# Strassen's scheme for the input projections of the feed-forward stage: seven products of quarters in place of eight

## The chip, the cores and the metric

The kernel runs on one core of a Trainium2 chip. The metric is the time of one execution on the device, in microseconds (us); lower is better. The five engines are named as the profile names them: PE (TensorE, matrix products; PEld is its loading of weights), DVE (VectorE), ACT (ScalarE), POOL (GpSimd) and SP (SyncE, which here only issues transfers). Every engine works through its own list of instructions in order and waits on semaphores for the others.

## What is computed

The reference is one block of a hybrid model on 512 tokens of 1024 features, in float32. Three mixers (a gated linear recurrence, an RWKV-7 layer and a latent attention) are merged, and a gated feed-forward stage follows. Only that last stage is touched:

```python
h = rms_norm(x, ffn_pre_g[l])
gate, up = jnp.split(h @ w_ffn_in[l], 2, axis=-1)
x = x + rms_norm((jax.nn.silu(gate) * up) @ w_ffn_out[l], ffn_post_g[l])
```

Here `h` is 512 x 1024, `w_ffn_in` is 1024 x 5632 (2816 columns of gate, then 2816 of up), and `w_ffn_out` is 2816 x 1024.

## The kernel before

**Three products for one.** Each float32 operand is split into a high part, rounded to the format `float32r` in which PE takes it, and a low part, the rest. `mm3` (L134 to L139) then issues three matmuls for one: high by high (L137), high by low (L138), low by high (L139). The tokens' operand `h` is split once and stays on the chip (`self.h`: eight tiles `xH` and eight `xL`, each 128 features x 512 tokens). The weights are split as they come: `slab` (L196) loads 256 KB into a staging tile `wsD`, ACT casts it to the high tile `whD` (L205), and DVE subtracts for the low tile `wlD` (`split_low`, L132). `wsD`, `whD` and `wlD` have three buffers each, so at most three slabs of weights are ready or in use.

**The streaming loop.** `stream` (L210) takes 256 columns of weights, that is two feature tiles of 128, against all 1024 features of the input: four slabs, and for each of them two columns x two feature rows x three matmuls of 512 tokens, 12 matmuls in all. The results gather in two tiles `mmD` of the accumulation memory (PSUM), of which the pool `pD` has four. A helper, `lane`, gives instructions a priority class; the order on each engine is then made when the program is built, by a list scheduler that simulates the engines. Lane 0 is the most urgent.

**The stage in question** is `ffn` (L1240). It has eleven pairs of feature tiles (22 tiles of 128 make 2816). For each pair a stream of gate columns and one of up columns are run, 96 matmuls of 512 tokens. Then comes the gating: ACT takes a tanh of the gate (L1256), DVE forms (1 + tanh) x gate (L1257) and the product with up (L1261), ACT writes the high part `fH` (L1262) and DVE the low part `fL` (L1263). The first pair is different: its four streams take half of the tokens each (256), so that it can start while `h` for the other half is still being made by the stage ahead (`to_fm`: transposes on PE at L357, `xH` on ACT at L360, `xL` on DVE at L361).

**What follows** is `project` (L1205) with `w_ffn_out`: slabs of 128 rows x 512 columns through the same `slab` (staging tiles `wsD` again), accumulated in four tiles `po`. Beside it the residual `x1` is loaded from memory (L1281) into tiles called `xH0` to `xH7` in the pool `hp`, which are the buffers of the high tiles of `h`, so those loads wait until the last matmul that reads `h` is done. The gain `gp` is loaded at the start of `ffn` (L1246 and L1247).

Outside this stage POOL does small work: a token (L149) per group of matmuls, which paces the streams of the earlier stages and is off in `ffn`, powers for the norms (L279), and a few elementwise operations in the mixers (L594, L717).

## Time and profile before

| | |
|---|---|
| median of 3 runs | 1403.33 us (1401.97 to 1404.83) |
| the profiled execution, whole | 1408.42 us |
| its span, first to last instruction | 1406.6 us |
| granted clock of PE over the span | 0.996 |
| PE busy | 1354.8 us (96%) |
| DVE busy | 848.3 us (60%) |
| ACT busy | 638.6 us (45%) |
| POOL busy | 190.8 us (14%) |

A busy time is the time in which at least one instruction of the engine runs. PE's matmuls overlap: each is shown with its own length, and the next one starts well before it ends, so what a matmul costs is read from the distance of starts, not from its length. In the rows of groups, `out<-in` names the tiles without their buffer numbers, then the shapes, the count, the busy time and the mean length in ns, and at the end the idle time of the engine ahead of these instructions with what ended it. A timeline row has the start in us, the length in us, the engine, the line, the operation and, as xN, how many instructions were merged into the row.

### The profile page before, as it was taken

Reading aid. Unit: us, or ns where it says so; the run is one execution under the profiler, and the core shown is the slowest. Engines: PE = TensorE matmul, PEld = TensorE weight load, DVE = VectorE, ACT = ScalarE, POOL = GpSimd, SP = SyncE. Lnnn points to the kernel's source line nnn. Section 1 sums busy time; section 2 is a strip of 40 time slices with the busy share of each in tenths; the row PEclk is TensorE's granted clock in tenths of the full one; section 3 lists DMA queues with packets and bytes.
Section 4 is the critical chain, followed back from the end, with each engine's and each line's share of the span. In section 5 each row is a group of like instructions: output and inputs, shape, how many; then the busy total and the mean of one; then the engine's idle time right before and its main releaser. Section 6 shows DMA issues by size and latency. Waiting matters only on the chain.

```text
span 1406.6 us, 27356 instructions
## 1 busy us (share of the span) xinstructions
PE 1354.8 (96%) x9664; PEld 1103.2 (78%) x9664; DVE 848.3 (60%) x1756; ACT 638.6 (45%) x1259; POOL 190.8 (14%) x1042
## 2 busy tenths in 40 slices
PE   6999999999999999999999999999999999999998
PEld 5777777777777777888788888877888888888886
DVE  5567797797787784575665576655575344343234
ACT  5554546556556453433665354443354333332222
POOL 2122132131222311242210000001010000000000
PEclk9999999999999999999999999999999999999999
DMA  5565467557755777986464555415544333334233
GB/s 180 149 193 144 129 183 227 178 153 218 213 157 155 242 237 227 356 277 208 137 204 147 157 178 168 130 53 173 198 139 135 98 97 92 102 95 156 97 98 105
DMA packets 196025, 231.62 MB, mean 165 GB/s; under 512 B 42672, under 2 KB 137392, under 8 KB 195888
## 3 DMA queue, kind: packets, MB, share of 16 engines
q1 hardware_dynamic: 194496, 226.72, 52.1%
q10 hardware_dynamic: 1392, 3.15, 0.7%
q8 instruction: 76, 1.25, 0.4%
q14 instruction: 61, 0.50, 0.1%
HBM read 169.65 MB, written 60.16 MB: 163 GB/s over the span
## 4 chain that ended last, share of the span: by engine, by line
PE 82%; DMA 6%; DVE 4%; issue 4%; ACT 3%; POOL 1%; SPq 1%; POOLq 0%; DVEq 0%; ACTq 0%
PE mmD L137 18%; PE mmD L138 17%; PE mmD L139 17%; PE po L137 4%; PE po L139 4%; PE po L138 4%; PE pr L194 1%; DMA wsD<-in_w_in_dram 1%; DMA z<-zst 1%; DMA zr<-z 1%; PE pmo L1138 1%; PE pm L137 1%; PE pm L139 1%; PE pm L138 1%; PE ph L843 1%
## 5 line engine op out<-in xcount | busy, mean ns | idle before, releaser
L137 PE MATMUL mmD<-xH,whD 128*128 128x512 f32 (+1 forms) x1232 | 486.2, 397 | 11.9 <-POOL token L149 5.6
L138 PE MATMUL mmD<-xL,whD 128*128 128x512 f32 (+1 forms) x1232 | 474.2, 386 | 0.0
L139 PE MATMUL mmD<-xH,wlD 128*128 128x512 f32 (+1 forms) x1232 | 469.6, 385 | 0.9 <-DVE wlD L132 0.9
L132 DVE TENSOR_TENSOR wlD<-wsD,whD 128x512 fp32r<-128x512 f32 x384 | 263.2, 687 | 292.0 <-ACT whD L205 276.0
L205 ACT CAST whD<-wsD 128x512 fp32r<-128x512 f32 x384 | 236.7, 618 | 375.8 <-PE mmD L138 244.1
L137 PEld LDWEIGHTS mmD<-xH,whD 128*128 128x128 f32 x1232 | 232.0, 189 | 65.2 <-POOL token L149 8.9
L139 PEld LDWEIGHTS mmD<-xH,wlD 128*128 128x128 f32 x1232 | 232.2, 189 | 48.6 <-DVE wlD L132 2.0
L138 PEld LDWEIGHTS mmD<-xL,whD 128*128 128x128 f32 x1232 | 233.5, 190 | 40.1
L149 POOL MEMSET token<- 1x1 f32 x912 | 82.2, 90 | 675.4 <-PE mmD L139 660.1
L139 PE MATMUL po<-whD,fL 128*128 128x512 f32 x176 | 68.6, 390 | 0.0
L138 PE MATMUL po<-wlD,fH 128*128 128x512 f32 x176 | 68.6, 390 | 0.0
L137 PE MATMUL po<-whD,fH 128*128 128x512 f32 x176 | 61.9, 390 | 0.0
L279 POOL TENSOR_TENSOR rrs<-rtm,mhalf 128x1 f32<-128x1 f32 x8 | 4.4, 551 | 402.3 <-DVE rtm L274 368.7
L646 DVE TENSOR_TENSOR invtmp<-inv 64x30 f32<-64x30 f32 (+14 forms) x120 | 38.7, 322 | 17.7 <-DMA inv<-Ld 16.0
L594 POOL TENSOR_SCALAR BK<-BK,gC 128x128 f32<-128x128 f32 x56 | 47.0, 854 | 11.8 <-PE pr L194 11.8
L237 ACT COPY zst<-mmD 128x512 f32<-128x512 f32 x64 | 37.3, 583 | 14.6 <-PE mmD L139 14.4
L647 DVE TENSOR_TENSOR inv<-inv,invtmp 64x30 f32<-64x30 f32 (+14 forms) x120 | 38.4, 320 | 2.2
L139 PEld LDWEIGHTS po<-whD,fL 128*128 128x128 f32 x176 | 33.0, 188 | 7.0
L138 PEld LDWEIGHTS po<-wlD,fH 128*128 128x128 f32 x176 | 33.0, 188 | 7.0
L137 PEld LDWEIGHTS po<-whD,fH 128*128 128x128 f32 x176 | 33.0, 188 | 7.0
L843 PEld LDWEIGHTS ph<-hq,hk 128*32 128x32 f32 x1536 | 17.6, 111 | 18.0 <-issue 9.6
L1136 ACT COPY mpT<-pmt 128x128 f32<-128x128 f32 (+3 forms) x32 | 13.6, 425 | 38.0 <-PE pmt L1134 37.9
(349 smaller groups left out, 1960.1 us busy)
## 6 DMA issues: line engine op xcount, KB each, us to landing
wsD<-in_w_in_dram SPq DMA_DIRECT2D x176, 256.0 KB, 3.4
wsD<-in_w_ffn_in_dram SPq DMA_DIRECT2D x96, 256.0 KB, 2.8
z<-zst SPq DMA_DIRECT2D x63, 256.0 KB, 3.3
rwd<-G SPq DMA_DIRECT2D x28, 512.0 KB, 5.5
G<-rwd SPq DMA_DIRECT2D x28, 512.0 KB, 6.7
wsD<-in_w_branch_dram SPq DMA_DIRECT2D x48, 256.0 KB, 2.9
wsD<-in_w_ffn_out_dram SPq DMA_DIRECT2D x44, 256.0 KB, 2.6
zr<-z SPq DMA_DIRECT2D x26, 256.0 KB, 3.3
```

Of the source, the lines that this page charges most:

```text
L132: (eng or self.nc.vector).tensor_tensor(dst, src, high.bitcast(F32), op=ALU.subtract)
L137: first = mm(ps, lhsT=lh, rhs=rh, start=start, stop=False)
L138: mm(ps, lhsT=lh, rhs=rl, start=False, stop=False)
L139: return first, mm(ps, lhsT=ll, rhs=rh, start=False, stop=stop)
L149: token = self.nc.gpsimd.memset(self.token, 0.0).ins
L194: last = c()
L205: nc.scalar.copy(h, st)
L237: self.nc.scalar.copy(st[:m], ps)
L594: Pl.tensor_scalar(BK[:, c], BK[:, c], gC[:, c + 1:c + 2], None, op0=ALU.mult)
L646: V.tensor_tensor(tv, cv, rv, op=ALU.mult)
L647: V.tensor_tensor(U[:, :j, j + 1:], U[:, :j, j + 1:], tv, op=ALU.add)
L843: mm(g[b:b + HB, o // P, :], lhsT=k[:, t], rhs=q[:, t], start=True, stop=True)
```

## The change

The first pair stays as it was (moved to `ffn_first`, with other scratch tiles). The other ten pairs are each computed as one 2 x 2 block product: the rows of the block are gate and up (256 columns of weights each), the inner index is the lower and upper half of the 1024 features, and the columns are the two halves of the tokens. Winograd's form of Strassen's scheme takes seven products of quarters where the plain form has eight, with sums of weights (s1 to s4), sums of tokens' operands (T1 to T4) and sums of the results. Each product is 512 features x 256 columns by 256 tokens: two slabs, each with 12 matmuls of 256 tokens.

- `ffn_sides` forms T1 to T4 once: POOL adds high and low parts back (16 operations of 128x256), DVE subtracts four times (128x1024), and the results are split again by ACT and DVE. T4 is written over the right halves of the first four `h` tiles. Its scratch tiles are the buffers into which the weights of the first Strassen pair are then loaded (tags `wg0`, `wg1`, `wu0`, `wu1`).
- `ffn_seven` runs once per pair. It loads the four quarters of the weights, 512 KB each, into four tiles of which only `wu0` has two buffers. POOL forms s1 to s4 (four operations of 128x1024). Then come seven products, each with ACT's cast and DVE's split of two slabs, seven sums of results on DVE with one operand in PSUM, a copy on ACT, and the gating in two halves of the tokens, whose product with up is now on POOL.
- The results' sums lie in the staging tiles `wsD`. The gain `gp` and what `project` needs now come from a pool `fo`, opened when the tiles of the Strassen pairs are closed.

```diff
-        for f in range(0, KF, 2):
-            ts_ = [self.t(fp, [P, S], f"ft{j}", bufs=2) for j in range(2)]
...
-            if f:
-                self.stream(wg, self.h, gate)
-                self.stream(wu, self.h, up)
...
+            self.ffn_first(fH, fL, win)
+            T = self.ffn_sides(fin)
+            for f in range(2, KF, 2):
+                self.ffn_seven(fin, fH, fL, win, T, f)
+        fo = es.enter_context(tc.tile_pool(name="fo", bufs=1))
+        gp = self.t(fo, [P, D], "gp")
...
+    def ffn_sides(self, fin):
...
+                    Pl.tensor_tensor(q[:, j], self.h[0][4 * k + j][:, c].bitcast(F32),
+                                     self.h[1][4 * k + j][:, c].bitcast(F32), op=ALU.add)
...
+        def side(n, dst, a, b):
+            V.tensor_tensor(dst, a, b, op=ALU.subtract)
...
+            A.copy(h, dst)
+            self.split_low(l, dst, h)
...
+        side(1, B[0, 0], B[0, 1], B[0, 0])
+        side(3, B[0, 1], B[1, 1], B[0, 1])
+        side(2, B[1, 1], B[1, 1], B[0, 0])
+        side(4, B[1, 0], B[1, 1], B[1, 0])
...
+    def ffn_seven(self, fin, fH, fL, win, T, f):
...
+        a11, a21, a22, a12 = load("wg0", 0, 0), load("wu0", 1, 0, 2), load("wu1", 1, 1), load("wg1", 0, 1)
+        s1, s2, s4 = (self.t(fin, [P, 4, 2 * P], n) for n in ("ws1", "ws2", "ws4"))
+        Pl.tensor_tensor(s1, a21, a22, op=ALU.add)
+        Pl.tensor_tensor(s2, s1, a11, op=ALU.subtract)
+        s3 = a21
+        Pl.tensor_tensor(s3, a11, a21, op=ALU.subtract)
+        Pl.tensor_tensor(s4, a12, s2, op=ALU.subtract)
...
+        def product(w, x):
+            ps = self.t(self.pD, [P, 2, N], "mmD")
+            for k0 in range(0, 4, 2):
+                h, l = (self.t(self.wd, [P, 2, 2 * P], t, F32R, 3) for t in ("whD", "wlD"))
...
+                A.copy(h, w[:, k0:k0 + 2])
+                self.split_low(l, w[:, k0:k0 + 2], h)
...
+            A.activation(t, gate, AF.Tanh, scale=0.5)
+            V.scalar_tensor_tensor(t, t, 1.0, gate, op0=ALU.add, op1=ALU.mult)
+            Pl.tensor_tensor(t, t, up, op=ALU.mult)
+            A.activation(fH[:, f:f + 2, tok], t, AF.Copy, scale=0.5)
+            V.scalar_tensor_tensor(fL[:, f:f + 2, tok], t, 0.5, fH[:, f:f + 2, tok].bitcast(F32),
+                                   op0=ALU.mult, op1=ALU.subtract)
...
+        soon(A.copy, m1, product(a11, b11))
+        add(u2, m1, product(s2, t2))
+        m4 = product(a22, t4)
+        m5 = product(s1, t1)
+        add(u3, u2, product(s3, t3))
+        add(c22, u3, m5)
+        soon(V.tensor_tensor, u3, u3, m4, op=ALU.subtract)
+        add(u2, u2, m5)
+        add(m1, m1, product(a12, b21))
+        gated(0, m1, u3)
+        add(u2, u2, product(s4, b22))
+        gated(1, u2, c22)
```

Called in this order, the seven products are named P1 (a11), P2 (s2), P3 (a22), P4 (s1), P5 (s3), P6 (a12) and P7 (s4) below.

**Where the order moves.** Line numbers of rows of the changed kernel are its own: L1366 and L132 are the cast and the split of a Strassen slab, L1351 to L1355 the four sums of weights, L1384 the sums of results, L1392 to L1395 the gating, L1346 the loads of weights, L1263 the loads of `x1`.

DVE, in the middle of the stage, before: the row of splits, with the gating of one pair among them (`ft` is the gating's scratch, `mmD` the tile in PSUM).

```order
L132 TENSOR_TENSOR wlD_14015<-wsD_14012,whD_14014 128x512
L1263 SCALAR_TENSOR_TENSOR fL_12699<-ft_2490_13813,fH_12698 128x512
L132 TENSOR_TENSOR wlD_14033<-wsD_14030,whD_14032 128x512
L132 TENSOR_TENSOR wlD_14057<-wsD_14054,whD_14056 128x512
L132 TENSOR_TENSOR wlD_14075<-wsD_14072,whD_14074 128x512
L1257 SCALAR_TENSOR_TENSOR ft_2519_13972<-ft_2519_13972,mmD_13974 128x512
L132 TENSOR_TENSOR wlD_14093<-wsD_14090,whD_14092 128x512
L1257 SCALAR_TENSOR_TENSOR ft_2520_13973<-ft_2520_13973,mmD_13975 128x512
```

DVE at the same place in the changed kernel, from the first split of one pair (P1, of `wg_2540`) to the sum with its P2; `ws_2545` is s2, `wu_2542` is a22, `zst` is the gating's scratch of the pair before it, `c` and `wsD` hold sums of results.

```order
L132 TENSOR_TENSOR wlD_14158<-wg_2540_14137,whD_14157 128x512
L132 TENSOR_TENSOR wlD_14174<-wg_2540_14137,whD_14173 128x512
L1392 SCALAR_TENSOR_TENSOR zst_14091<-zst_14091,wsD_13882 128x512
L1384 TENSOR_TENSOR wsD_13883<-wsD_13883,mmD_14097 128x512
L132 TENSOR_TENSOR wlD_14192<-ws_2545_14146,whD_14191 128x512
L132 TENSOR_TENSOR wlD_14208<-ws_2545_14146,whD_14207 128x512
L1392 SCALAR_TENSOR_TENSOR zst_14131<-zst_14131,wsD_13883 128x512
L1395 SCALAR_TENSOR_TENSOR fL_12699<-zst_14091,fH_12698 128x2x256
L132 TENSOR_TENSOR wlD_14226<-wu_2542_14141,whD_14225 128x512
L132 TENSOR_TENSOR wlD_14242<-wu_2542_14141,whD_14241 128x512
L1384 TENSOR_TENSOR wsD_14153<-wsD_14152,mmD_14190 128x512
L1395 SCALAR_TENSOR_TENSOR fL_12699<-zst_14131,fH_12698 128x2x256
```

A pair has 25 DVE operations now where it had 14, and the last gating steps of one pair stand among the splits of the next: the split for P3 comes behind `fL` of the pair before.

POOL, the last four rows of the stage ahead and the first of the final norm, before: nothing lies between them.

```order
L279 TENSOR_TENSOR nrs_12523<-ntm_12522,mhalf 128x1
L279 TENSOR_TENSOR nrs_12636<-ntm_12635,mhalf 128x1
L279 TENSOR_TENSOR rrs_12628<-rtm_12627,mhalf 128x1
L279 TENSOR_TENSOR nrs_12636<-ntm_12635,mhalf 128x1
L279 TENSOR_TENSOR rrs_15396<-rtm_15395,mhalf 128x1
```

POOL between these places in the changed kernel, for one pair in the middle of the stage: the sums s1 to s4 of a pair (`ws_2592`, `ws_2593`, `wu_2589`, `ws_2594`), and the gating products (`zst`) around them.

```order
L1393 TENSOR_TENSOR zst_14091<-zst_14091,wsD_13884 128x512
L1393 TENSOR_TENSOR zst_14131<-zst_14131,c_2502_13885 128x512
L1351 TENSOR_TENSOR ws_2592_14415<-wu_2589_14409,wu_2590_14411 128x1024
L1352 TENSOR_TENSOR ws_2593_14416<-ws_2592_14415,wg_2588_14407 128x1024
L1354 TENSOR_TENSOR wu_2589_14409<-wg_2588_14407,wu_2589_14409 128x1024
L1355 TENSOR_TENSOR ws_2594_14417<-wg_2591_14413,ws_2593_14416 128x1024
L1393 TENSOR_TENSOR zst_14361<-zst_14361,wsD_14154 128x512
L1393 TENSOR_TENSOR zst_14401<-zst_14401,c_2550_14155 128x512
```

All four sums of the next pair stand ahead of the two gating products of the current one (`zst_14361` belongs to the pair whose splits are shown above).

SP, from the end of the stage on, before: the loads of `w_ffn_out` and of `x1` alternate.

```order
L201 DMA wsD_14637<-in_w_ffn_out_dram 128x512
L201 DMA wsD_14655<-in_w_ffn_out_dram 128x512
L1281 DMA xH_2639_14612<-x1d 128x512
L1281 DMA xH_2640_14613<-x1d 128x512
L201 DMA wsD_14673<-in_w_ffn_out_dram 128x512
L1281 DMA xH_2641_14614<-x1d 128x512
L1281 DMA xH_2642_14615<-x1d 128x512
```

SP at the same place in the changed kernel, from the last load of a quarter of `w_ffn_in` on.

```order
L1346 DMA wg_2783_15493<-in_w_ffn_in_dram 128x4x256
L1263 DMA xH_2829_15763<-x1d 128x512
L1263 DMA xH_2830_15764<-x1d 128x512
L1263 DMA xH_2831_15765<-x1d 128x512
L1263 DMA xH_2832_15766<-x1d 128x512
L1263 DMA xH_2833_15767<-x1d 128x512
L1263 DMA xH_2834_15768<-x1d 128x512
L1263 DMA xH_2835_15769<-x1d 128x512
L1263 DMA xH_2836_15770<-x1d 128x512
L201 DMA wsD_15788<-in_w_ffn_out_dram 128x512
L201 DMA wsD_15806<-in_w_ffn_out_dram 128x512
```

All eight loads of `x1` now stand ahead of the first load of `w_ffn_out`.

More of the change, by code (lines that the diff above doesn't have):

```diff
@@ L1287, in done, with ffn_first, gate, up @@
                 nc.sync.dma_start(self.out[0, i * P:(i + 1) * P, c], x1[i][n])
-        self.project(fp, po, (fH, fL), ins["w_ffn_out"][0], KF, gp, done, 6)
+        self.project(fo, po, (fH, fL), ins["w_ffn_out"][0], KF, gp, done, 6)
+    def ffn_first(self, fH, fL, win):
+        nc = self.nc
+        V, A = nc.vector, nc.scalar
+        ts_ = [self.t(self.wd, [P, S], "zst") for _ in range(2)]
+        def gate(j, pg):
+            t = ts_[j]
+            A.activation(t, pg, AF.Tanh, scale=0.5)
+            V.scalar_tensor_tensor(t, t, 1.0, pg, op0=ALU.add, op1=ALU.mult)
+        def up(j, pu):
+            t = ts_[j]
+            V.tensor_tensor(t, t, pu, op=ALU.mult)
+            A.activation(fH[:, j], t, AF.Copy, scale=0.5)
+            V.scalar_tensor_tensor(fL[:, j], t, 0.5, fH[:, j].bitcast(F32), op0=ALU.mult, op1=ALU.subtract)
+        wg, wu = win[:, :, :2 * P], win[:, :, DFF:DFF + 2 * P]
+        a, b = slice(0, S // 2), slice(S // 2, S)
+        pg = self.stream(wg, self.h, None, a)
+        pu = self.stream(wu, self.h, None, a)
+        self.stream(wg, self.h, gate, b, pg)
+        self.stream(wu, self.h, up, b, pu)
@@ new lines, in ffn_seven, with load, soon, gated @@
+    def ffn_seven(self, fin, fH, fL, win, T, f):
+        nc = self.nc
+        V, A, Pl = nc.vector, nc.scalar, nc.gpsimd
+        N = S // 2
+        def load(tag, row, k, bufs=1):
+            t = self.t(fin, [P, 4, 2 * P], tag, bufs=bufs)
+            nc.sync.dma_start(t, win[:, 4 * k:4 * k + 4, row * DFF + f * P:row * DFF + (f + 2) * P])
+            return t
+        a11, a21, a22, a12 = load("wg0", 0, 0), load("wu0", 1, 0, 2), load("wu1", 1, 1), load("wg1", 0, 1)
[5 more added lines that the diff above has]
+        Pl.tensor_tensor(s4, a12, s2, op=ALU.subtract)
+        xs = [[self.h[p][k][:, c * N:(c + 1) * N] for k in range(KD)] for c in range(2) for p in range(2)]
+        b11, b21, b22 = ([xs[0][:4], xs[1][:4]], [xs[0][4:], xs[1][4:]], [xs[2][4:], xs[3][4:]])
+        t1, t2, t3, t4 = (T[n] for n in (1, 2, 3, 4))
+        def product(w, x):
+            ps = self.t(self.pD, [P, 2, N], "mmD")
+            for k0 in range(0, 4, 2):
+                h, l = (self.t(self.wd, [P, 2, 2 * P], t, F32R, 3) for t in ("whD", "wlD"))
+                cur = self.cur_lane
+                self.lane(0)
+                A.copy(h, w[:, k0:k0 + 2])
+                self.split_low(l, w[:, k0:k0 + 2], h)
+                self.lane(cur)
+                for j in range(2):
+                    c = slice(j * P, (j + 1) * P)
+                    for k in range(2):
+                        first = k0 + k == 0 and j == 0
+                        self.mm3(ps[:, j], h[:, k, c], l[:, k, c], x[0][k0 + k], x[1][k0 + k],
+                                 first, k0 + k == 3 and j == 1)
+            return ps
+        small = lambda tag, bufs: self.t(self.wd, [P, 2, 2 * P], tag, bufs=bufs)
+        m1, u2, u3 = (small("wsD", 3) for _ in range(3))
+        cur = self.cur_lane
+        def soon(fn, *args, **kw):
+            self.lane(0)
+            fn(*args, **kw)
+            self.lane(cur)
+        def gated(c, gate, up):
+            t = self.t(self.wd, [P, S], "zst").rearrange("p (j n) -> p j n", j=2)
+            tok = slice(c * N, (c + 1) * N)
+            self.lane(0)
+            A.activation(t, gate, AF.Tanh, scale=0.5)
[4 more added lines that the diff above has]
+                                   op0=ALU.mult, op1=ALU.subtract)
+            self.lane(cur)
+        c22 = self.t(fin, [P, 2, N], "c22", bufs=2)
+        add = lambda dst, a, b: soon(V.tensor_tensor, dst, a, b, op=ALU.add)
+        soon(A.copy, m1, product(a11, b11))
[10 more added lines that the diff above has]
+        gated(1, u2, c22)
```

43 lines of the change are left out of this document (25 added, 18 removed).

## The prediction, made before the changed kernel was run

> **What bounds the kernel now.** The page comes first, then the stretches of the stage and its neighbours: start and end, then busy time and count on PE, PEld, DVE, ACT and POOL, then granted clock.
>
> ```profile
> PE 1354.8 (96%) x9664; PEld 1103.2 (78%) x9664; DVE 848.3 (60%) x1756; ACT 638.6 (45%) x1259; POOL 190.8 (14%) x1042
> 1038.00:1061.60 23.60, 22.69 (x191) 22.40 (x190) 16.43 (x29) 14.05 (x28) 0.02 (x1) 1.00 0.59 169
> 1061.60:1279.10 217.50, 217.50 (x962) 180.16 (x962) 94.34 (x143) 72.62 (x122) 0.00 (x0) 1.00 0.36 105
> 1279.10:1406.60 127.50, 120.51 (x530) 99.04 (x528) 42.55 (x69) 32.23 (x60) 2.19 (x4) 0.99 0.31 104
> ```
>
> The second stretch is the ten pairs. PE never stops in it, DVE is busy 43%, ACT 33%, POOL not at all. 217.5 us for ten pairs is 21.75 us each, and for 960 matmuls 0.2266 us each. What PE does is the time here, so fewer products could shorten it. The price of the narrower matmul is in the timeline at the end of the first pair, whose streams are 256 tokens wide.
>
> ```profile
> 1059.86 0.28 PE L137 MATMUL mmD<-xH,whD 128*128 128x256 f32 x1
> ...
> 1061.54 0.28 PE L139 MATMUL mmD<-xH,wlD 128*128 128x256 f32 x1
> 1061.66 0.40 PE L137 MATMUL mmD<-xH,whD 128*128 128x512 f32 x1
> 1061.89 0.40 PE L138 MATMUL mmD<-xL,whD 128*128 128x512 f32 x1
> ```
>
> From the first to the last of these 256-wide matmuls lie 14 steps in 1.68 us: 0.120 us each, more than half of 0.2266.
>
> **PE's own part.** A pair had 96 matmuls of 512 tokens; it gets 7 x 24 = 168 of 256. 168 x 0.120 = 20.16 us against 21.75: 1.6 us a pair, 16 us for ten, if PE stays the bound. The one eighth of the work would be 27 us; 11 of them go into the narrower matmul. The section "Back-to-back issue gap" of "TensorE: Matmul & The Clock Gate" in the Trainium skill gives N/2.4 + 2.5 ns for an isolated matmul, 109 ns for 256 and 216 ns for 512; an estimate by that page is 20.7 against 18.3 us a pair, 8 us more gain in all. The steps in this trace are longer at both widths, and the measurement decides.
>
> **What the other engines get.** The rows that price it:
>
> ```profile
> L132 DVE TENSOR_TENSOR wlD<-wsD,whD 128x512 fp32r<-128x512 f32 x380 | 261.0, 688 | 289.2 <-ACT whD L205 273.2 <-PE mmD L138 14.5 <-DMA th<-gth 0.6
> L205 ACT CAST whD<-wsD 128x512 fp32r<-128x512 f32 x380 | 234.7, 620 | 369.2 <-PE mmD L138 244.1 <-PE po L139 72.5 <-issue 14.5
> L1261 DVE TENSOR_TENSOR ft<-ft,mmD 128x512 f32<-128x512 f32 x22 | 15.0, 687 | 9.1 <-PE mmD L139 9.1
> L785 DVE TENSOR_TENSOR y<-y,lnm 128x1024 f32<-128x1024 f32 x4 | 4.9, 1224 | 0.1
> L717 POOL TENSOR_TENSOR St<-PV,gC 64x512 f32<-64x512 f32 x12 | 13.0, 1082 | 17.0 <-DVE PV L743 10.2 <-DVE PV L741 6.3
> ```
>
> A slab now feeds 12 matmuls of 0.120, so it lasts 1.44 us where it lasted 2.72, and 14 slabs go through ACT and DVE per pair instead of 8. DVE per pair: 14 splits and two `fL` have both inputs in SBUF, 16 x 0.688 = 11.0 us; seven sums and two gate steps have one input in PSUM, 9 x 0.687 = 6.2 us; together 17.2 of 20.16. ACT: 14 x 0.62, and five more of about 0.6: 11.7 us, hidden. POOL had nothing; the nearest row for its sums is L717, 512 elements in 1.08 us, so 128x1024 is taken as 2.16 and the gating product as 1.08: 4 x 2.16 + 2 x 1.08 = 10.8 us. Each engine fits below 20.16 alone. Whether DVE and POOL can run together is another matter. The longest L868 (DVE, two inputs in SBUF) and the place where it occurred:
>
> ```profile
> L868 DVE TENSOR_TENSOR hk<-hk,hF x48: 409/418/1290, 133.5 to 645.1; 128x256 f32<-128x256 f32 x48
> 603.60 2.26 POOL L717 TENSOR_TENSOR St<-PV,gC 64x512 f32<-64x512 f32 x2 [2.20 <-DVE PV L743]
> 604.27 0.30 DVE L854 COPY_PREDICATED hsd<-hgm,ph 128x128 f32<-128x128 uint8 x1
> 604.48 0.46 DVE L867 TENSOR_TENSOR hq<-hq,hf 128x256 f32<-128x256 f32 x1
> 604.86 1.29 DVE L868 TENSOR_TENSOR hk<-hk,hf 128x256 f32<-128x256 f32 x1
> 195.35 3.71 POOL L594 TENSOR_SCALAR BK<-BK,gC 128x128 f32<-128x128 f32 x3 [0.73 <-PE pr L194]
> L594 POOL TENSOR_SCALAR BK<-BK,gC x56: 593/604/2934, 75.8 to 483.5; 128x128 f32<-128x128 f32 x56
> ```
>
> L868 needs 0.42 us. Here it started while the second L717 ran and ended at 606.15, 0.29 us after POOL's end at 605.86: it stood still until POOL was done. L854, with one input in PSUM, was not held. The other way round, three L594 of 0.6 us each took 3.71 us under a row of DVE operations. So they exclude each other, and either may wait. The section "Who interferes with whom" of "SBUF — State Buffer" in the Trainium skill says the same: a DVE instruction with two SBUF inputs contends with a GpSimd instruction that reads SBUF, for its whole length, and order of issue decides. It speaks against this change, and this trace agrees (1290 against 418 ns).
>
> Per pair POOL's 10.8 us and DVE's 11.0 us cannot overlap: 21.8 us, more than PE's 20.16 and as much as the old pair. A second ring ties POOL to the transfers. All of the next pair's s1 to s4 stand ahead of this pair's gating products on POOL, and s4 waits for a12, whose one buffer is free only after the split of P6. Transfers:
>
> ```profile
> wsD<-in_w_ffn_in_dram SPq DMA_DIRECT2D x96, 256.0 KB, 2.8
> wsD<-in_w_ffn_out_dram SPq DMA_DIRECT2D x44, 256.0 KB, 2.6
> x<-in_x_dram SPq DMA_DIRECT2D x4, 512.0 KB, 5.6
> ```
>
> A quarter of 512 KB lies between 2.8 and 5.6 us; I take the middle, 4.2. The ring: s1, s2, s3 with a DVE split let in between each, 3 x 2.16 + 3 x 0.62 = 8.4; a12 lands, 4.2; s4, 2.2; gating product, 1.1; ACT's `fH` and DVE's `fL`, 1.4; the two splits of P3, which stand behind `fL` on DVE, 1.3; then a22's buffer is free, and its transfer, 4.2, lets the next s1 start: 22.8 us. While `fL` waits, every later split waits behind it, and PE has three slabs, 4.3 us, to live on. Bounds for a pair: 20.2 (PE alone, all waits hidden by the three slabs) and 28.0 (DVE never beside POOL, 17.2 + 10.8). I take 22.4, between the sum of 21.8 and the ring of 22.8.
>
> **The start.** DVE's last operations of the first pair, before, and SP and PE at the end of the stage:
>
> ```profile
> 1051.46 0.69 DVE L132 TENSOR_TENSOR wlD<-wsD,whD 128x512 fp32r<-128x512 f32 x1 [0.57 <-ACT whD L205]
> 1059.13 0.68 DVE L1257 SCALAR_TENSOR_TENSOR ft<-ft,mmD 128x512 f32<-128x512 f32 x1
> 1278.80 1.00 SPq L1281 DMA_DIRECT2D xH<-x1d  x2
> 1279.29 0.39 PE L137 MATMUL po<-whD,fH 128*128 128x512 f32 x1
> L361 DVE SCALAR_TENSOR_TENSOR xL<-tr,vT,xH 128x256 fp32r<-128x256 f32 x32 | 14.3, 477 | 3.2 <-ACT xH L360 3.2
> ```
>
> Between 1050.9 and a22's first load DVE must now do five splits (3.4), four `xL` (1.9), two gate steps (1.4) and seven operations of T1 to T4 of 1.22 (8.5): 15.2 us, to 1066.1. T2's split is the last reader of the buffer that a22 needs. Then a22 lands (4.2), POOL forms s1 and s2 (4.3), ACT casts and DVE splits (1.3): P2 starts at 1075.9. Without waits it would start at 1061.66 + 2.88 = 1064.5. So the start costs 11.4 us. The bounds: 8.6 us earlier if the T operations fill DVE's idle time in the first pair (23.60 - 16.43 = 7.2) and the transfer takes 2.8; 4 us later if the eight POOL sums of the second half of `h` (0.54 each) hold DVE too.
>
> **The end.** Before, the first `po` matmul followed the last `mmD` at once. Now the eight loads of `x1` stand ahead of the first slab of `w_ffn_out` on SP, and the last two wait for P7's last matmul, since `xH6` and `xH7` are read until then. Two loads take 1.0 us to issue, the slab lands in 2.6, cast and split take 1.3: 4.9 us in which PE has nothing (0 if the order did not matter, which the waits exclude; 8 if the slab lands in 5.6). The later load of `gp` is covered: its first reader comes after 22 slabs of 12 matmuls of 0.2266, 60 us later. The last gating runs beside the first slabs; its tiles are needed only at the end of the sum over k.
>
> **The sum.** P2 starts at 1075.9; the rest of its pair is 6/7 x 22.4 = 19.2; nine pairs are 201.6; the stage ends at 1296.7, 17.6 after 1279.1; with 4.9 the loss is 22.5 us. The profiled execution took 1408.42, its span 1406.6; what lies outside, 1.8, stays, and so does all else. On the median of the runs, 1403.3 + 22.5 = 1426 us. The break-even is a pair of 20.1 us: just PE's own pace. 0.2%, 2.8 us, is about what a measurement can tell from no change.
>
> **Rivals.**
>
> 1. POOL gives way, and PE stays the bound. For it: in the L594 rows it is POOL that waited, and a split can be done 1.6 us before PE needs it (two slabs ahead, 2.88, less cast and split, 1.31). Against it: the L868 rows, and that port demand exceeds 20.16. A pair is then 20.2: 1075.9 + 17.3 + 181.8 = 1275.0, 4.1 earlier, less 4.9: 1404. If the start also loses only 4 us (P2 at 1069), 1397: faster. It decides for faster when the pairs stay at PE's pace and P2 starts before 1072.
> 2. The ring of POOL and transfers sets the pace. With quarters landing in 5.6 us it is 22.8 + 2 x 1.4 = 25.6 a pair; P2 starts at 1077.3, the stage ends at 1077.3 + 21.9 + 230.4 = 1329.6, 50.5 later, with 4.9: 1459. For it: 5.6 is the only load of that size from the inputs. Against: that load ran at the very start beside others, and this stage has half of that traffic.
>
> **How the numbers follow.** The forecast, a pair of 21 to 24.5 us (1412 to 1447, by the same sum), gets 0.56. Rival 1 gets 0.24: half of that faster by over 0.2%, a third within 0.2%, the rest slower. Rival 2 gets 0.20. Faster 0.12, same 0.08, slower 0.80. The range leaves out some 0.09 at the fast end and about half of rival 2: 1399 to 1453.
>
> **What would show it.** In the profile of the changed kernel: starts of 256-wide matmuls 0.120 apart inside a slab; 21 to 24.5 us from pair to pair; PE idle, released by ACT's casts and DVE's splits; some L132 lengthened to 1.5 or 2.5 us while a POOL sum runs; POOL sums above 2.16 us; P2's first matmul some 11 us late; some 5 us without PE ahead of the first `po`. If no split of DVE is ever lengthened and the pairs take 20.2 us, the exclusion was the wrong step. If the pairs take over 25 us, the transfers or the order on POOL were worse than I made them.

## The result and the profile after

The changed kernel takes 1473.84 us (median of 4 runs, 1473.59 to 1474.18), the kernel before, run beside it, 1404.08 (4 runs, 1401.97 to 1405.75): 1.0498 times as long, 95% interval 1.0480 to 1.0516. It is slower, as forecast, but by 70 us and not by 23, and the stated range ended at 1453. The profiled execution took 1473.59 us, its span 1471.8.

The page's first part, and then the stretches of the stage: the first pair, the time from it to P2 of the second pair, the rest of the Strassen pairs, and what follows. The columns are start and end, then length, busy time and count on PE, PEld, DVE, ACT and POOL, then granted clock, DMA share, GB/s.

```profile
PE 1364.6 (93%) x10384; PEld 1139.1 (77%) x10384; DVE 1011.1 (69%) x1877; ACT 683.2 (46%) x1336; POOL 339.8 (23%) x1118
```

```profile
1038.00:1061.80 23.80, 22.80 (x186) 22.18 (x185) 20.41 (x31) 15.25 (x30) 13.25 (x15) 0.98 0.53 156
1061.80:1077.80 16.00, 7.63 (x42) 6.73 (x41) 10.66 (x18) 6.30 (x13) 5.40 (x3) 0.74 0.43 131
1077.80:1336.70 258.90, 218.92 (x1656) 210.19 (x1656) 240.48 (x244) 108.76 (x183) 124.80 (x56) 0.96 0.25 77
1336.70:1471.80 135.10, 121.88 (x529) 100.03 (x528) 44.60 (x72) 34.22 (x63) 5.12 (x6) 0.96 0.34 112
```

In the third stretch, which is P2 to P7 of one pair and nine whole pairs (9.857 pairs), PE stands still for 40 us, and DVE counts as busy in 240.5 of 258.9 us, 93%. DVE has become the engine that paces the stage. 258.9 by 9.857 is 26.3 us a pair. The same comes out of a landmark that occurs once a pair, the second gating product on POOL, in the timeline: eight pairs lie between these two rows, 211.55 us, 26.44 each. All "pairs" below are measured in this way.

```profile
1107.86 1.68 POOL L1393 TENSOR_TENSOR zst<-zst,c 128x512 f32<-128x512 f32 x1 [1.83 <-DVE zst L1392]
1319.41 1.68 POOL L1393 TENSOR_TENSOR zst<-zst,c 128x512 f32<-128x512 f32 x1 [1.83 <-DVE zst L1392]
```

What DVE does in these 26 us is in the groups of the stretch, with busy us, then mean ns of one: its splits by the weights that they read (`wg` holds a11 and a12, `wu` a22 and s3, `ws` s1, s2 and s4), and POOL's sums s1 to s4 and the gating products.

```profile
L132 DVE TENSOR_TENSOR wlD<-wg,whD 128x512 fp32r<-128x512 f32 x38 | 78.8, 2111 | 1.5 <-ACT whD L1366 1.5
L132 DVE TENSOR_TENSOR wlD<-wu,whD 128x512 fp32r<-128x512 f32 x40 | 52.4, 1330 | 13.9 <-ACT whD L1366 13.6
L132 DVE TENSOR_TENSOR wlD<-ws,whD 128x512 fp32r<-128x512 f32 x60 | 49.9, 850 | 6.2 <-ACT whD L1366 5.8
...
L1351 POOL TENSOR_TENSOR ws<-wu,wu 128x1024 f32<-128x1024 f32 x9 | 22.7, 2523 | 45.3 <-DVE wlD L132 20.7 <-DMA wu<-in_w_ffn_in_dram 15.1 <-issue 9.5
L1352 POOL TENSOR_TENSOR ws<-ws,wg 128x1024 f32<-128x1024 f32 x10 | 26.9, 2685 | 0.8
L1354 POOL TENSOR_TENSOR wu<-wg,wu 128x1024 f32<-128x1024 f32 x10 | 27.8, 2785 | 0.0
L1355 POOL TENSOR_TENSOR ws<-wg,ws 128x1024 f32<-128x1024 f32 x10 | 24.2, 2416 | 39.5 <-DVE wsD L1384 21.2 <-DMA wg<-in_w_ffn_in_dram 18.4
```

The same split took 0.688 us before. Held time is what lies above that: 38 x 1.42 + 40 x 0.64 + 60 x 0.16 = 89.5 us, 9.1 us a pair. DVE's own work is the rest of its busy time, (240.5 - 89.5) / 9.857 = 15.3 us a pair, and 1.9 us it is idle. 15.3 + 9.1 + 1.9 = 26.3. A stretch of the timeline shows how the holding goes; the second column is the duration.

```profile
1193.74 2.41 POOL L1351 TENSOR_TENSOR ws<-wu,wu 128x1024 f32<-128x1024 f32 x1 [5.75 <-DVE wlD L132]
1194.15 2.55 DVE L132 TENSOR_TENSOR wlD<-wu,whD 128x512 fp32r<-128x512 f32 x1 [0.75 <-ACT whD L1366]
...
1196.23 2.72 POOL L1352 TENSOR_TENSOR ws<-ws,wg 128x1024 f32<-128x1024 f32 x1
...
1196.62 5.66 DVE L132 TENSOR_TENSOR wlD<-wg,whD 128x512 fp32r<-128x512 f32 x2
...
1198.91 2.83 POOL L1354 TENSOR_TENSOR wu<-wg,wu 128x1024 f32<-128x1024 f32 x1
1199.55 0.39 PE L139 MATMUL mmD<-xH,wlD 128*128 128x256 f32 x1 [1.11 <-DVE wlD L132]
...
1202.21 0.68 DVE L1384 TENSOR_TENSOR wsD<-wsD,mmD 128x512 f32<-128x512 f32 x1
```

From 1194.15 to 1202.3, while s1, s2 and s3 run back to back on POOL, DVE gets three splits done, one for each sum: 8.1 us for 2 us of work. Each split ends about half a microsecond after the sum that it stood beside, and is followed at once by the next that stands. Behind them on DVE stood operations with one input in PSUM (L1384); these took 0.67 to 0.69 us on the mean, here and in every run below. PE had its three slabs, 4.3 us, to live on, and ran dry at 1198.4.

### The profile page after: what moved, and what is told of

Its sections match the earlier page's. It is cut to its first block, busy times and chain, and to the rows that moved or that the text cites. A ratio compares the mean times of both kernels' runs of the same rounds, so it can differ in the third digit from the quotient of the medians.

```text
span 1471.8 us, 29118 instructions
## 1 busy us (share of the span) xinstructions
PE 1364.6 (93%) x10384; PEld 1139.1 (77%) x10384; DVE 1011.1 (69%) x1877; ACT 683.2 (46%) x1336; POOL 339.8 (23%) x1118
## 4 chain that ended last, share of the span: by engine, by line
PE 67%; DVE 13%; DMA 7%; issue 7%; ACT 3%; POOL 1%; SPq 1%; DVEq 0%; POOLq 0%; ACTq 0%
PE mmD L137 14%; PE mmD L139 13%; PE mmD L138 13%; DVE wlD L132 7%; PE po L137 4%; PE po L138 4%; PE po L139 4%; DMA wsD<-in_w_in_dram 2%; PE pr L194 1%; DMA z<-zst 1%; PE pmo L1138 1%; PE pm L137 1%; PE pm L139 1%; PE pm L138 1%; DVE wsD L1384 1%
## 5 line engine op out<-in xcount | busy, mean ns | idle before, releaser
L139 PE MATMUL mmD<-xH,wlD 128*128 128x512 f32 (+1 forms) x1232 | 446.1, 365 | 40.7 <-DVE wlD L132 40.7
L137 PE MATMUL mmD<-xH,whD 128*128 128x512 f32 (+1 forms) x1232 | 455.7, 372 | 14.1 <-POOL token L149 5.9
L138 PE MATMUL mmD<-xL,whD 128*128 128x512 f32 (+1 forms) x1232 | 444.5, 362 | 0.0
L132 DVE TENSOR_TENSOR wlD<-wsD,whD 128x512 fp32r<-128x512 f32 (+1 forms) x304 | 208.9, 689 | 185.7 <-ACT whD L205 170.2
L205 ACT CAST whD<-wsD 128x512 fp32r<-128x512 f32 (+1 forms) x304 | 187.2, 618 | 261.6 <-PE mmD L138 125.0
L132 DVE TENSOR_TENSOR wlD<-wg,whD 128x512 fp32r<-128x512 f32 x40 | 80.1, 2040 | 1.5 <-ACT whD L1366 1.5
L1366 ACT CAST whD<-ws 128x512 fp32r<-128x512 f32 x60 | 36.9, 616 | 71.1 <-PE mmD L138 63.4
L132 DVE TENSOR_TENSOR wlD<-wu,whD 128x512 fp32r<-128x512 f32 x40 | 52.4, 1330 | 13.9 <-ACT whD L1366 13.6
L132 DVE TENSOR_TENSOR wlD<-ws,whD 128x512 fp32r<-128x512 f32 x60 | 49.9, 850 | 6.2 <-ACT whD L1366 5.8
L1366 ACT CAST whD<-wg 128x512 fp32r<-128x512 f32 x40 | 24.7, 620 | 45.0 <-PE mmD L138 42.5
L237 ACT COPY zst<-mmD 128x512 f32<-128x512 f32 x64 | 37.3, 583 | 15.6 <-PE mmD L139 15.3
```

Source lines behind the costliest of these rows:

```text
L132: (eng or self.nc.vector).tensor_tensor(dst, src, high.bitcast(F32), op=ALU.subtract)
L137: first = mm(ps, lhsT=lh, rhs=rh, start=start, stop=False)
L138: mm(ps, lhsT=lh, rhs=rl, start=False, stop=False)
L139: return first, mm(ps, lhsT=ll, rhs=rh, start=False, stop=stop)
L205: nc.scalar.copy(h, st)
L237: self.nc.scalar.copy(st[:m], ps)
```

## The experiments

**The theories.** A: DVE and POOL exclude each other whenever DVE reads two inputs from SBUF, and DVE, being in order, loses nearly the whole length of each sum. B: the transfers and the order of buffers around POOL set the pace (the second rival of the prediction, whose 1459 us come closest to the result). Each kernel was timed beside the kernel before on one chip (medians of 1406 to 1409 us there), and the second number of each result is the ratio to it. The changed kernel itself was not timed beside the experiments, so where a time is set against its 1473.84 us, a few us tell nothing. The places in the stage come from one profiled execution each, and the stage does not begin at the same time in all of them: the first matmul of its first pair, ahead of everything that was changed, starts between 1027.04 us (run 3) and 1035.05 (run 7). The starts of P2 are therefore compared by their distance from this matmul, 44.16 us in the changed kernel.

**1. One input of the split in PSUM.** The split subtracts a PSUM tile that holds zeros, instead of the high part in SBUF; DVE and POOL issue as much as they did.

```diff
-                self.split_low(l, w[:, k0:k0 + 2], h)
+                V.tensor_tensor(l, w[:, k0:k0 + 2], self.zero, op=ALU.subtract)
```

> The DVE splits of the ten Strassen pairs take their second input from a PSUM tile of zeros in place of the high part in SBUF; the low parts are then not the rests, so this leaves out the right low part. Count and length of DVE's instructions stay, POOL's work stays, the order stays. Theory A (a DVE instruction with two SBUF inputs and a POOL sum exclude each other for the whole of an instruction, and that alone sets the pair at 26.4 us): no split longer than 0.8 us, DVE busy per pair down from 25 to about 16 us, pairs of 20.2 to 21.5 us, time 1410 to 1428. Theory B (the ring of POOL's order and the transfers of a12 and a22 sets the pair): the ring is untouched but for the splits let in between, pairs of 24 to 26 us, time 1450 to 1470.

Measured: 1411.73 us, 1.0030 times before (1.0005 to 1.0055). The groups, the stretch of the pairs, and the landmark:

```profile
L1370 DVE TENSOR_TENSOR wlD<-wu,po 128x512 fp32r<-128x512 f32 x39 | 26.6, 682 | 13.0 <-PE mmD L139 13.0
L1370 DVE TENSOR_TENSOR wlD<-wg,po 128x512 fp32r<-128x512 f32 x38 | 25.2, 683 | 15.1 <-PE mmD L139 15.1
...
L1357 POOL TENSOR_TENSOR wu<-wg,wu 128x1024 f32<-128x1024 f32 x9 | 21.7, 2415 | 0.0
```

```profile
1077.00:1277.00 200.00, 199.68 (x1649) 199.47 (x1647) 159.47 (x242) 106.92 (x181) 111.90 (x56) 0.99 0.33 100
```

```profile
1098.61 1.29 POOL L1396 TENSOR_TENSOR zst<-zst,c 128x512 f32<-128x512 f32 x1 [1.46 <-DVE zst L1395]
1259.89 1.29 POOL L1396 TENSOR_TENSOR zst<-zst,c 128x512 f32<-128x512 f32 x1 [1.43 <-DVE zst L1395]
```

Splits beside a sum of 2.4 us take 0.68, PE is busy in 199.7 of 200 us, and a pair takes 161.28 / 8 = 20.16: to the hundredth what 168 matmuls of 0.120 give. The transfers, the buffers and the order on POOL are as in the changed kernel. So theory A carries the pairs, and B falls as the main cause. One more thing goes with this edit: the split no longer reads the high part, so it does not wait for ACT's cast either (the rows above wait for PE; in the changed kernel DVE waited 21 us for the cast in the stretch, 2.1 a pair). Run 11, where every split needs ACT's work first again, shows that the hold was what counted. That a DVE instruction with one SBUF input is not held is what the section "Who interferes with whom" of "SBUF — State Buffer" in the Trainium skill states; this run agrees, 0.68 us beside POOL's 2.41.

**2. Fewer transfers.** a22 and a12 are loaded for the first Strassen pair and kept.

```diff
-        a11, a21, a22, a12 = load("wg0", 0, 0), load("wu0", 1, 0, 2), load("wu1", 1, 1), load("wg1", 0, 1)
+        a11, a21 = load("wg0", 0, 0), load("wu0", 1, 0, 2)
+        if f == 2:
+            self.kept = load("wu1", 1, 1), load("wg1", 0, 1)
+        a22, a12 = self.kept
```

> The quarters a22 and a12 are loaded for the first Strassen pair only and used for all ten; this leaves out 18 loads of 512 KB, so nobody waits for a buffer of these two and for its transfer (3.5 us each in the changed kernel). Theory A: pairs stay within 1 us of 26.4, time 1464 to 1475. Theory B: the two transfers go out of the ring, pairs fall by 3 to 7 us, time 1405 to 1445.

Measured: 1458.81 us, 1.0367 (1.0341 to 1.0393), 15 us less than the changed kernel; a pair takes 24.96 us, 1.5 less. That lies between the two expectations and in neither range. DVE is held as before: its splits of `wu` took 1.96 us on the mean and those of `wg` 1.57, and from 1090 to 1280 us held time is 9.3 us a pair. What fell is DVE's idle time, from 1.9 to 0.5 us a pair. So transfers and the wait for their buffers have a small part in the loss.

**3. Sums in halves.** Each POOL sum is issued as two of 512 elements.

```diff
-        Pl.tensor_tensor(s1, a21, a22, op=ALU.add)
+        for c in (slice(0, 2), slice(2, 4)):
+            Pl.tensor_tensor(s1[:, c], a21[:, c], a22[:, c], op=ALU.add)
```

> The four POOL sums of weights of a pair are cut into two instructions of 128x512 each, same result. Theory A in the form that the port time adds up (POOL's time plus DVE's time, whatever the pieces): no gain, 26 to 27.5 us a pair, time 1470 to 1485. Theory A in the form that the single long wait hurts (2.4 us against three slabs of 1.44 us): single waits of DVE halve, pairs of 23 to 25 us, time 1440 to 1462. Theory B: POOL's chain is a little longer by eight fixed costs instead of four, 1473 to 1482.

Measured: 1446.83 us, 1.0282 (1.0226 to 1.0338), from two executions 12 us apart, 1440.76 and 1452.90; a pair takes 23.73 us in the first of them, the profiled one. The groups that are held, and a half sum:

```profile
L132 DVE TENSOR_TENSOR wlD<-wg,whD 128x512 fp32r<-128x512 f32 x34 | 45.8, 1373 | 3.4 <-ACT whD L1370 3.2
L132 DVE TENSOR_TENSOR wlD<-ws,whD 128x512 fp32r<-128x512 f32 x51 | 43.0, 868 | 0.0
L132 DVE TENSOR_TENSOR wlD<-wu,whD 128x512 fp32r<-128x512 f32 x36 | 38.5, 1087 | 11.4 <-ACT whD L1370 11.4
...
L1357 POOL TENSOR_TENSOR wu<-wg,wu 128x512 f32<-128x512 f32 x16 | 28.7, 1793 | 0.0
L1396 DVE SCALAR_TENSOR_TENSOR zst<-zst,wsD 128x512 f32<-128x512 f32 x16 | 19.6, 1227 | 0.0
```

Held time per pair: 4 x 0.69 + 6 x 0.18 + 4 x 0.40 + 2 x 0.54 = 6.5 us, 2.6 less than in the changed kernel; the pair is 2.7 shorter. The number of elements that POOL adds is the same, and POOL is busy for longer. So it is not POOL's time on the port that adds up; what counts is how much of it DVE spends standing, and that falls with the length of one POOL instruction.

**4. Sums on DVE.** s1 to s4 go to DVE, at the most urgent priority.

```diff
-        Pl.tensor_tensor(s1, a21, a22, op=ALU.add)
+        V.tensor_tensor(s1, a21, a22, op=ALU.add)
```

> The four sums of weights move from POOL to DVE (128x1024 in 1.22 us each), same result; POOL keeps the gating products. Theory A: DVE has 25 x 0.605 + 4 x 1.14 = 19.7 us a pair and waits only for the two gating products, pairs of 21 to 22.5 us, P2 of the first Strassen pair 2 us earlier, time 1415 to 1435. Theory C (DVE simply has too many instructions, and the port is a side matter): DVE gets 4.6 us more, pairs of 27 us or more, time above 1475.

Measured: 1439.81 us, 1.0232 (1.0211 to 1.0253); a pair takes 23.26 us; both are above what was expected. P2 comes 41.97 us after the first matmul of the stage, 2.2 sooner, as expected. DVE gets 4 x 1.22 = 4.9 us of work more, and the kernel is 34 us faster than with POOL's help. What is left to hold DVE is POOL's gating product: `fL` took 1.23 us on the mean. Held time is 1.7 us a pair (from 1090 to 1280 us, the splits of `ws` counted in), DVE's own work 19.8 and its idle time 1.7.

**5. A real second input in PSUM.** ACT copies the cast weights of 12 of the 14 slabs a second time, into idle PSUM banks, and the split reads that copy.

```diff
+                    A.copy(g, h.bitcast(F32))
+                    V.tensor_tensor(l, w[:, k0:k0 + 2], g, op=ALU.subtract)
```

> ACT copies the cast weights of 12 of a pair's 14 slabs a second time, into PSUM banks that lie idle in this stage, and DVE's split takes that copy as its second input; all else as after the change. Nothing of the computation is left out. Theory A (a POOL sum holds DVE only while DVE reads two inputs from SBUF): the 12 splits stay at 0.68 to 0.75 us beside POOL's sums, a pair takes 20.4 to 21.5 us, and the time is 1412 to 1425 us; ACT gets 12 x 0.62 = 7.4 us a pair more and is then at about 19 of 20.5. Rival (the hand-over from ACT to DVE, or ACT itself, is what cannot keep up with a slab of 1.44 us): a pair takes 23 us or more, 1437 us and up.

Measured: 1444.27 us, 1.0246 (1.0221 to 1.0271), 30 us under the changed kernel and some 20 above what theory A had led me to expect; a pair takes 23.24. Both numbers are in the rival's range, so this run alone does not decide between the two. All twelve splits take 0.68. But the gate step, which has both inputs in SBUF, is now the one that stands beside s4:

```profile
L1398 DVE SCALAR_TENSOR_TENSOR zst<-zst,wsD 128x512 f32<-128x512 f32 x18 | 30.1, 1672 | 0.9
```

```profile
1167.97 2.73 POOL L1355 TENSOR_TENSOR ws<-wg,ws 128x1024 f32<-128x1024 f32 x1 [1.49 <-DVE wlD L1373]
...
1168.36 2.90 DVE L1398 SCALAR_TENSOR_TENSOR zst<-zst,wsD 128x512 f32<-128x512 f32 x1
1171.18 0.68 DVE L132 TENSOR_TENSOR wlD<-wg,whD 128x512 fp32r<-128x512 f32 x1
```

The split at 1171.18 is one that PE waits for, and it stands behind the gate step in the queue. Held time is 2 x 0.98 for the gate steps, 2 x 0.36 for `fL` (1.05 us on the mean) and 0.2 for the splits of a11, 2.9 us a pair; the pair is 3.1 over PE's pace, although DVE is busy in no more than 168 of 210 us:

```profile
1090.00:1300.00 210.00, 189.24 (x1520) 183.56 (x1519) 168.04 (x226) 161.35 (x281) 114.33 (x54) 1.00 0.29 88
```

**6. x1 after the first slabs.** The loads of `x1` are issued after the sixth slab of `w_ffn_out`.

```diff
-        for i in range(NT):
-            for n in range(2):
-                nc.sync.dma_start(x1[i][n], x1d[i][:, n * 512:(n + 1) * 512])
+                if late and n == 0 and k == 5:
+                    late()
```

> The eight loads of x1 are issued after the sixth slab of w_ffn_out instead of ahead of the first; all else as after the change. If those loads ahead of the slab are the cause of the pause in front of the first po matmul (6.2 us), it falls to under 1.5 us and the time to 1467 to 1470 us. If the pause comes from the last gating products and their splits, it stays at 4 us or more, and the time above 1471 us.

Measured: 1471.13 us, 1.0442 (1.0421 to 1.0464). SP's own queue shows that the edit did not get them out of the way:

```profile
1320.28 13.76 SPq L1266 DMA_DIRECT2D xH<-x1d  x8
1334.12 30.77 SPq L201 DMA_DIRECT2D wsD<-in_w_ffn_out_dram  x14
```

The scheduler still put all eight ahead of the first slab. The pause ahead of the first `po` was 5.37 us (6.20 in the changed kernel). A second thing is seen here: the gate step of DVE, which frees one of the three buffers `wsD` that the first slab needs, ended at 1333.52, 0.6 us before that slab was issued:

```profile
1332.83 0.69 DVE L1395 SCALAR_TENSOR_TENSOR zst<-zst,wsD 128x512 f32<-128x512 f32 x1 [0.70 <-ACT zst L1394]
```

In runs 9 to 11, where the gates no longer sit in a `wsD` buffer, the pause is 2.55 to 2.63 us, against 4.07 in run 8. Run 9 differs from run 8 in that, in one PSUM bank less for the copies, and in the order on SP (five loads of `x1` ahead of the first slab and not six). So 1.5 us of the pause are probably the buffers'; the part of the loads of `x1` was not separated. Run 12 is the only one with no more than four of these loads ahead of the first slab, which is issued there 7.9 us before the first `po`; its pause is 0.7 us.

**7. Earlier loads at the start.** The sums of the halves of `h` lie in the buffers of the weight sums, so that the first four quarters can be loaded early.

```diff
+                tag = {(0, 0): "ws2", (0, 1): "ws1", (1, 1): "ws4", (1, 0): "wu0"}[k, t]
-                q = B[k, t] = self.t(fin, [P, 4, N], tag + str(t), bufs=2 if (k, t) == (1, 0) else 1)
+                q = B[k, t] = self.t(fin, [P, 4, N], tag, bufs=2 if (k, t) == (1, 0) else 1)
```

> The sums of the two halves of x, from which T1 to T4 are made, lie in the buffers of the weight sums (and one spare quarter), no longer in those of the first four quarters, which can so be loaded some 10 us earlier; all else as after the change. If the first pair's late start comes from the late buffer of a22 and its transfer, P2 starts at 1071 to 1074 us instead of 1077.8, and the time is 1466 to 1471 us. If DVE's work on T1 to T4 alone sets it, P2 stays at 1076 to 1078 us, and the time at 1472 to 1475 us.

Measured: 1473.56 us, 1.0461 (1.0438 to 1.0484): a miss in time. P2 starts at 1076.36 us, but the stage itself began later in this execution. The first matmul of the first pair, in the changed kernel and here:

```profile
1033.66 0.47 PE L137 MATMUL mmD<-xH,whD 128*128 128x256 f32 x2 [1.53 <-DVE rs L1236]
```

```profile
1035.05 0.47 PE L137 MATMUL mmD<-xH,whD 128*128 128x256 f32 x2 [1.53 <-DVE rs L1236]
```

From there to P2 are 44.16 us in the changed kernel and 41.31 here: the edit won 2.9 us, less than the 4 to 7 expected. The timeline of POOL and DVE there:

```profile
1068.18 3.88 POOL L1352 TENSOR_TENSOR ws<-wu,wu 128x1024 f32<-128x1024 f32 x1 [7.15 <-DVE T3L L132]
```

```profile
1073.13 7.31 DVE L132 TENSOR_TENSOR xL<-wu,xH 128x256 fp32r<-128x256 f32 x4
```

s1 starts 5.5 us earlier than in the changed kernel by the same measure (33.13 us after that matmul, 38.66 there), and now falls among DVE's operations on T1 to T4: s1 takes 3.88 us, and four splits of T4 (1.43 us together in the changed kernel) 7.31. So about half of what the earlier transfer won was lost again in a collision. The time shows nothing of the 2.9 us, but differences of this size from the changed kernel are not clear.

**8. The three together.**

> The second copy in PSUM, the late x1 loads and the buffers of the start together; nothing of the computation is left out. If the loss is the exclusion of DVE and POOL plus the start plus the end, as theory A has it, pairs of 20.4 to 21.5 us, P2 at 1071 to 1074 and no pause at the end give 1401 to 1415 us, level with the kernel before (1404 to 1408), as far as PE alone can bring it: 10 x 1.5 us gained, less some 8 at the start. If it stays above 1425, something else holds the pairs.

Measured: 1444.12 us, 1.0255 (1.0232 to 1.0278), like run 5; P2 at 1071.64, 40.98 us after the first matmul of the stage, pairs 23.24. As the last clause of the expectation says, something else held the pairs: the gate step of run 5.

**9. The gates in PSUM as well.**

```diff
-        add(m1, m1, product(a12, b21))
-        gated(0, m1, u3)
+        add(g0, m1, product(a12, b21))
+        gated(0, g0, u3)
```

> The three edits of the run before together, and the two sums that feed the gates are written to a PSUM bank, so that the gate step on DVE no longer has both inputs in SBUF (it took 1.67 us on the mean there, one in two 2.90 beside a POOL sum, against 0.68); nothing of the computation is left out. Theory A (each DVE operation with two SBUF inputs waits for the whole POOL sum, and what stands behind it on DVE waits too): the gate steps fall to 0.68 to 0.75 us, the pairs from 23.4 to 20.6 to 21.8 us, and the time from 1444 to 1412 to 1428 us. Rival (DVE waits for ACT's second copy, 36 us of waits in nine pairs, and these two hand-overs set the pace): the pairs stay at 23 us or more and the time at 1436 us or more.

Measured: 1435.51 us, 1.0202 (1.0179 to 1.0224); a pair takes 22.62. The gate steps took 0.68 us, as theory A had it, but the time is above its range: the next operation in the queue with two SBUF inputs, the second split of a11, took the gate step's place beside s4. The rival's bounds (23 us, 1436 us) are missed by little, so neither expectation is met.

```profile
1168.24 2.74 POOL L1359 TENSOR_TENSOR ws<-wg,ws 128x1024 f32<-128x1024 f32 x1 [1.31 <-DVE wlD L1377]
```

```profile
1168.62 0.68 DVE L1402 SCALAR_TENSOR_TENSOR zst<-zst,po 128x512 f32<-128x512 f32 x1
1169.22 2.30 DVE L132 TENSOR_TENSOR wlD<-wg,whD 128x512 fp32r<-128x512 f32 x1
```

**10. The same with halves** (the diffs of 9 and 3).

> The same with each POOL sum in two halves of 512; nothing of the computation is left out. Theory A: what is left to hold are the two splits of a11 and the two fL, which took 0.81 and 1.05 us on the mean; with halves they wait for less, but POOL works longer: within 4 us of the run beside it, 1410 to 1428 us. Rival: no change in the pairs, 1436 us or more for both.

Measured: 1424.31 us, 1.0118 (1.0101 to 1.0135), 11 us under run 9; a pair takes 21.40. The time is in theory A's range, but run 9 is not within 4 us of it, as had been expected. The held split falls with the length of the sum, as in run 3 (splits of `wg` without a copy: 1.53 us on the mean in run 9, 0.97 here).

**11. Copies where POOL works.** The slabs without a copy are those of a22 and s1, whose splits run while POOL does nothing.

```diff
-                if w is a11:
+                if w is a22 or w is s1:
                     self.split_low(l, w[:, k0:k0 + 2], h)
```

> As the run with the halves, but the splits that get the second copy in PSUM are chosen by when they run: those of a22 and s1, which fall into the 7 us of a pair in which POOL does nothing, go without it (both inputs in SBUF), and those of a11, which had a split of 2.30 us beside a POOL sum, get it: 10 copies a pair instead of 12. Nothing of the computation is left out. Theory A: all splits at 0.68 to 0.80 us with fewer copies, pairs from 21.3 to 20.5 to 21.1 us, the time from 1424 to 1414 to 1422 us. Rival (the number of DVE operations with two SBUF inputs in a pair counts, not when they run): with two more of them the pairs lengthen to 21.8 us or more and the time to 1427 us or more.

Measured: 1413.94 us, 1.0053 (1.0035 to 1.0071). The splits without a copy, the stretch of the pairs, and the landmark:

```profile
L132 DVE TENSOR_TENSOR wlD<-wu,whD 128x512 fp32r<-128x512 f32 x18 | 11.5, 678 | 0.0
L132 DVE TENSOR_TENSOR wlD<-ws,whD 128x512 fp32r<-128x512 f32 x18 | 11.5, 678 | 0.0
```

```profile
1090.00:1280.00 190.00, 187.04 (x1531) 184.77 (x1532) 149.83 (x229) 151.73 (x261) 106.99 (x86) 1.00 0.30 93
```

```profile
1096.27 1.29 POOL L1407 TENSOR_TENSOR zst<-zst,c 128x512 f32<-128x512 f32 x1 [1.01 <-DVE zst L1406]
1263.13 1.30 POOL L1407 TENSOR_TENSOR zst<-zst,c 128x512 f32<-128x512 f32 x1 [1.00 <-DVE zst L1406]
```

Four splits a pair with both inputs in SBUF, none of them held, and a pair of 166.86 / 8 = 20.86 us, 5.6 under the changed kernel. So what costs is a two-input operation that meets a sum, not their number. The rival of runs 5 and 9 falls here too: from 1090 to 1280 us DVE waits 36.8 us for ACT's copies, 4.0 a pair, as in run 5 (32.9 us, 4.0 a pair), and yet the pair is 2.4 us shorter than there. The time is some 60 us under the changed kernel's, and still 7 us over that of the kernel before.

**12. P6 second.** P6, which needs no T, follows P1.

```diff
         soon(A.copy, m1, product(a11, b11))
+        p6 = product(a12, b21)
         add(u2, m1, product(s2, t2))
```

> The same, and P6, which needs no T, is the second product of a pair instead of the sixth, so that PE has 2.9 us more of work while T2 and s2 are made. Nothing of the computation is left out. If the first pair's late start is a plain wait for T2 and s2, PE's pause there shrinks by 2.9 us, the granted clock falls less, and the time is 3 to 6 us under the run beside it: 1409 to 1418 us. If the order of the products matters to the buffers of a12 and the gates instead, the pairs lengthen and the time is the same or above.

Measured: 1419.75 us, 1.0095 (1.0076 to 1.0113), slower than run 11: a miss. P2 starts 42.93 us after the first matmul of the stage, against 40.88 in run 11: 2.05 us later, with a product of 2.9 us put ahead of it. So 0.8 of the 2.9 us was won at the start. In run 11 PE's long wait, 4.58 us, lies inside P1 already, for a split of a11 that stands behind the work on the T's, and P2 itself waited only 0.36 us. The pairs lengthen to 22.2 us; why was not followed up.

The pairs and lengths in this table are those of the profiled executions; the times are medians. The two differ most in run 3 (profiled 1440.76 us) and in run 9 (1440.09).

| kernel | time, us | a pair, us | DVE operation held most (mean) |
|---|---|---|---|
| changed | 1473.84 | 26.44 | split of `wg`, 2.11 |
| 2, fewer loads | 1458.81 | 24.96 | split of `wu`, 1.96 |
| 3, halves | 1446.83 | 23.73 | split of `wg`, 1.37 |
| 4, sums on DVE | 1439.81 | 23.26 | `fL`, 1.23 |
| 5, copies in PSUM | 1444.27 | 23.24 | gate step, 1.67 |
| 9, gates in PSUM | 1435.51 | 22.62 | split of a11, 1.53 |
| 10, and halves | 1424.31 | 21.40 | split of a11, 0.97 |
| 11, copies chosen by time | 1413.94 | 20.86 | `fL`, 1.05 |
| 1, no split with two SBUF inputs | 1411.73 | 20.16 | `fL`, 1.01 |

## Why the prediction was wrong

The direction, the mechanism and its place were right. The size was not, and most of the error is in one term.

- **The pair: the step that failed.** The text took "22.4, between the sum of 21.8 and the ring of 22.8". The sum counted two operations too few: the gate steps were taken as reading PSUM, but in the changed kernel they read `zst` and `wsD`, both in SBUF, so that a pair has 18 such operations of DVE and seven with an input in PSUM. With the measured lengths, four sums at 2.41 and two gating products at 1.29 are 12.2 us of POOL, and 18 operations of DVE, which start 0.60 us apart when nothing holds them, are 10.8: 23.0 in place of 21.8. That is still 3.3 us short of the pair. The larger mistake was to take such a sum as a pace that could be reached. It would need DVE's seven operations with an input in PSUM to run while POOL works. DVE is in order, three sums come back to back, and at its head stands a split: POOL is busy for 12.7 us a pair (124.8 / 9.857), and for 9.1 us a pair DVE stood. So a pair is DVE's own 15.3, the 9.1, and 1.9 idle: 26.3. Over 9.857 pairs the error is 9.857 x (26.3 - 22.4) = 38 us of the 48. The text had the ingredient ("every later split waits behind it") and gave it to `fL` alone; the same holds for a split at the head of the queue. Its upper bound, 28.0 ("DVE never beside POOL"), describes best what came; the second rival's 25.6 is nearer as a number.
- **The three slabs of lead** were to cover a split's wait ("1.6 us before PE needs it"). They cover one; three held splits in a row, 8.1 us, they do not.
- **POOL's sums**: "2.16" was taken; unhindered they are 2.41 (run 1), beside DVE's splits up to 2.8. The text's sign of this ("POOL sums above 2.16") came.
- **The second rival** gave 1459, nearest of all numbers, for a reason that was wrong: quarters were to land in 5.6 us. They land in 3.5, less than the 4.2 of the forecast, and run 2 gives the transfers 1.5 us of a pair. That its time came close is chance. The text's sign, too, that pairs of over 25 us would mean transfers or POOL's order, misled: run 1 left both as they were, and the pair fell to 20.16.

```profile
wu<-in_w_ffn_in_dram SPq DMA_DIRECT2D x20, 512.0 KB, 3.5
```

- **The first rival** (POOL gives way) did not come: in the pairs POOL's sums grow from 2.41 to 2.8 us at most, while DVE's splits grow from 0.69 to 2.8. But its price was sound. With the exclusion taken away (run 1) the pairs take the 20.16 us that it counted on, and the time is 1411.7, where it had 1404: the start and the end eat the gain of PE.
- **The start**: P2 at 1077.82 us, forecast 1075.9, 1.9 late; 0.7 of that lies ahead of the stage, whose first matmul starts at 1033.66 us and not at 1032.98.

```profile
1077.82 0.58 PE L137 MATMUL mmD<-T2H,whD 128*128 128x256 f32 x1 [4.02 <-ACT whD L1366]
```

The chain that the text gave for it (the buffer of a22, its transfer, two sums) holds in the changed kernel. Freed of it (run 7), P2 comes 2.9 us sooner and no more, since s1 then meets DVE's work on T1 to T4.

- **The end**: PE pauses for 6.20 us ahead of the first `po`, forecast 4.9. All eight loads of `x1` stand ahead of the slab, as said; that a `wsD` buffer comes free hardly earlier (run 6), I had not seen.

```profile
1342.93 2.04 PE L137 MATMUL po<-whD,fH 128*128 128x512 f32 x4 [6.20 <-issue]
```

- **The sum.** The first `po` was forecast at 1301.6 us and came at 1342.93, 41.3 late: 1.9 of the start, 38.1 of the pairs, 1.3 of the end. About 1.5 us more came after it; from 1340 to 1350 us the granted clock was 0.70. The remaining 5 us to the 47.8 between the medians come from the profiled execution of before, which was 5 us above its median.
- **PE's own pace**, 0.120 us a matmul and 20.16 a pair, was right to the hundredth, and so was the narrowness of the gain: even with the exclusion nearly gone (run 11) seven products did not beat eight here, as the start and the end cost more than the pairs gain.

## What to carry to other kernels

Before work is given to GpSimd, count which VectorE operations with two SBUF inputs will meet it, and charge each meeting with the rest of the GpSimd instruction, and with all that stands behind it in VectorE's queue; a sum of the two engines' times (23.0 us here) was less than the pair took (26.3). The remedies that worked here are an input in PSUM, shorter GpSimd instructions, and placing the two-input operations where GpSimd is idle; when one held operation is cured, look for the next in the queue, since it takes the place. A scheme that saves an eighth of the products has to be priced at the narrower matmul's measured step, and its gain (16 us here) set against what its start and end cost.
